# Streams' states renewed in the second mixer, a seven-product down projection in ffn3, merged vector steps and identity products at the start

## The chip, the cores and the metric

The kernel runs on one core of a Trainium2 chip. The metric is the device time of one execution in microseconds (us); below 'the median' is that of three runs. TensorE (PE) multiplies, VectorE (DVE) and ScalarE (ACT) work elementwise, GpSimd (POOL) does small elementwise work and some DMAs, and SyncE (SP) issues nearly all other DMAs. Each engine takes its own instructions in order and waits on semaphores of the others.

## The reference

A streaming encoder of two layers, one inference step for 512 new frames of one stream and 16 frames for each of 8 running streams: 640 tokens of 1024 channels. Each sub-layer ends in `x <- LayerNorm(ALPHA * x + sublayer(x))`:

```python
swiglu:     (silu(x @ w_gate) * (x @ w_up)) @ w_down          # 1024 -> 2816 -> 1024, four times
mixer_ab:   S5 recurrence and stick-breaking attention        # first layer
mixer_ssd:  # second layer; per head r of a group g, 64 rows of state
    xbc  = silu(conv(xbc))                                    # 4 taps, per channel
    cs   = cumsum(dt * a)
    y    = (c @ b.T * exp(cs_t - cs_s) masked * dt) @ x + (c @ h) * exp(cs) + d * x
    h    = h * exp(cs[-1]) + (exp(cs[-1] - cs) * dt * b).T @ x    # new state
    yg   = y * silu(z);  yg = yg * rsqrt(mean(yg ** 2) + eps) * norm_g
    out  = yg @ w_out
```

The outputs are y, the new states of the S5 and SSD recurrences (`ssd_sample`: 8 streams x 32 heads x 64 x 128), keys, values and the last rows of the convolution.

## The kernel before, in words

The order of phases is ffn0, mix0 (first mixer), ffn1, ffn2, mix1 (second mixer), ffn3. Products are in fp32r, with each operand split into a high part and the rest: `split` lets ACT round (`L95`) and DVE subtract (`L96`), and `mm3` (`L134`) makes three products of the pairs. Weights come in pieces of 512 KB through SP into `raw`, are split into `w`, and are used up by PE.

In an FFN the gate and up products of pairs of row blocks f (128 of 2816) are taken by `pair` (`L358`), and `down` multiplies four f at a time into `yacc`. In ffn1 and ffn2 the first five chunks of four f go through `down7` (products `L494`): a two-by-two product of blocks by seven products in place of eight, for four of the five token tiles, with sums of rows (`row_sums`) and of weights on DVE and some results added by POOL's accumulating DMAs (`L506`). ffn0 and ffn3, and the last chunk of each FFN, take eight.

The second mixer works in 4 groups g of 8 heads. For each group six input projections (`xbc`: copy to `ext`, convolution `L1554` to `L1557`, tanh, `L1559`, to memory as `bcx_d`) and four gate projections (`gate_in`, to memory as `z_d`) come first; they are a group ahead of the recurrences and fill in between their steps. A step (g, c) is one token tile c: 4 (the eight running streams) first, then 0 to 3 (the long stream). `core_a` loads `bx` (b, c, x of the tile) and `csb` (the cumulated decay on all partitions), makes the decays (`L1662`, exp `L1664`, `L1670`) and takes b times c on PE (`L1666`, `L1667`). `core_b` multiplies with the running state and renews it (`L1701` to `L1719`); `core_s` does the same for the eight running streams, whose old states `h0` it loads (8 of 128x512 per group, two to a tile). `gate_out` of the group before follows: times z, norm, a split `og` (`L1780`, `L1781`) and 24 products with `w_out` per tile. After the last step only `gate_out(3, c)` and the layer norm are left.

The new states of the running streams are not made in the mixer: it leaves split x and b in memory (`xb_d`) and the decays (`el_d`). `ssd_states`, a generator that is stepped during ffn3, loads them again with h0, takes a product (`L1467`) per group and stream from `xrow` and `brow` (three parts of 16 rows, for two streams at a time, loaded by 12 DMAs), multiplies h0 by its decay and adds (`L1469`, `L1470`).

The order of the instructions on each engine is set when the program is built, by a scheduler that simulates the engines and takes what is ready first, in program order otherwise; `issue_after` pins an instruction behind another one. On the chip that order is fixed.

Of the kernel before, what the change touches and what calls it, by code (L numbers as in the profile page):

```python
# [21 lines left out]
T = 640  # L22
# [8 lines left out]
SEVEN = ("ffn1", "ffn2")  # L31
# [5 lines left out]
def kernel(ctx: ExitStack, tc: tile.TileContext, I, O, phases=PHASES):  # L37
# [31 lines left out]
    def bank_b():  # L69
        return bank("b")  # L70
# [58 lines left out]
    def mm3(ps, lhs, rhs):  # L129
        n = 3 * len(lhs)  # L130
        k = 0
        for (wh, wl), (xh, xl) in zip(lhs, rhs):
            for a, b in ((wh, xh), (wl, xh), (wh, xl)):
                state["pe"] = nc.tensor.matmul(ps, a, b, start=(k == 0), stop=(k == n - 1)).ins  # L134
                k += 1

# [76 lines left out]
    def ffn(i, ph, last, side=None):  # L213
# [4 lines left out]
        with ExitStack() as st:  # L218
# [3 lines left out]
            def tick(where):  # L222
# [1213 lines left out]
    ssd = {}  # L1436

# [5 lines left out]
    def ssd_states(wk):  # L1443

        el8 = wk.tile([128, 4, 8, 8], F32, name="el8")
        nc.sync.dma_start(el8.rearrange("p g b h -> p g (b h)"), ssd["el"])


        xrow = wk.tile([128, 512], F32R, name="xrow", bufs=1)
        brow = wk.tile([128, 2, 128], F32R, name="brow", bufs=1)  # L1450
        nc.vector.memset(xrow.bitcast(F32), 0.0)
        nc.vector.memset(brow.bitcast(F32), 0.0)
        for g, b2, q in ((g, b2, q) for g in range(4) for b2 in range(2) for q in range(2)):
            for h in range(2):
                for r, (sx, sb) in enumerate(((0, 0), (0, 1), (1, 0))):
                    rows = slice(64 * h + 16 * r, 64 * h + 16 * r + 16)
                    t0 = 64 * h + 32 * b2 + 16 * q
                    src = lambda s, a, b: ssd["xb"][g][s, t0:t0 + 16, a:b]
                    nc.sync.dma_start(xrow[rows].bitcast(F32), src(sx, 0, 512))
                    nc.sync.dma_start(brow[rows, h].bitcast(F32), src(sb, 512, 640))  # L1460
            for h in range(2):
                n = 4 * h + 2 * b2 + q
                h0 = wk.tile([128, 512], F32, name="h0", bufs=2)
                nc.sync.dma_start(h0, I["ssd_h0"][g, n])
                yield
                pst = bank_b()
# [520 lines left out]
```

## Time and profile before

| | |
|---|---|
| median of 3 runs | 2546.57 us (2545.01 to 2555.02) |
| profiled execution | 2548.97 us, its span 2547.3 us |
| PE / DVE / ACT / POOL busy | 2501.8 / 2017.0 / 1218.0 / 298.3 us |
| phases, from the span's start | ffn0 to 465.5, mix0 to 762, ffn1 to 1183, ffn2 to 1604.5, mix1 to 2110.2, ffn3 to the end |

Busy time counts an engine's instructions, not its waits. A group's row gives line, engine, operation, tiles, shapes, count, then busy time and the mean duration of one, then the idle time of the engine just before these instructions and what ended it. Matmuls overlap: their spacing, not the mean duration, is what one costs, and an fp32 matmul is two PE instructions.

### The profile page before, as it was taken

The numbers are of one execution on the slowest core, as the hardware profiler recorded it, in microseconds if no ns is written. First come the engines' busy times: TensorE is split into PE (matmuls) and PEld (weight loads), VectorE is DVE, ScalarE is ACT, GpSimd is POOL, SyncE is SP. The second block draws the span as 40 slices with busy tenths as digits, with TensorE's granted clock in tenths as the row PEclk, the third lists the DMA queues.
The fourth block names the chain that finished last, engine by engine and source line by source line (L and its number), as shares of the span: only waits on it lengthen the run. The fifth ranks groups of instructions, "written<-read, shape, count | busy, mean of one in ns | idle before, by whom it ended". The sixth has DMA issues, their size and how long they took to land. (4 is left out here: it accounts for less than half of the span.)

```text
span 2547.3 us, 40681 instructions
## 1 busy us (share of the span) xinstructions
PE 2501.8 (98%) x15577; PEld 2289.1 (90%) x15577; DVE 2017.0 (79%) x3685; ACT 1218.0 (48%) x2309; POOL 298.3 (12%) x432
## 2 busy tenths in 40 slices
PE   9999999999999999999999999999999999999998
PEld 8998999878789999999999999888989879999997
DVE  7787777676778888878888887777686799876768
ACT  4443344336744555553455554566565443443332
POOL 0000001210130000013000002311111150000001
PEclk9999999999999999999999999999999999999999
DMA  5322334443221433452144434366564722543442
GB/s 185 108 92 86 114 117 154 143 150 114 87 76 58 125 103 91 117 156 72 53 114 123 112 103 127 117 189 196 155 204 142 240 74 85 168 147 107 145 140 96
DMA packets 174835, 317.44 MB, mean 125 GB/s; under 512 B 20480, under 2 KB 91776, under 8 KB 174128
## 3 DMA queue, kind: packets, MB, share of 16 engines
q1 hardware_dynamic: 164816, 293.83, 36.2%
q0 software_dynamic: 9824, 21.01, 4.0%
q8 instruction: 122, 2.00, 0.3%
q14 instruction: 73, 0.60, 0.1%
HBM read 259.56 MB, written 40.54 MB: 118 GB/s over the span
## 5 line engine op out<-in xcount | busy, mean ns | idle before, releaser
L96 DVE TENSOR_TENSOR w<-raw,w 128x512 fp32r<-128x512 f32 (+1 forms) x601 | 524.1, 897 | 74.6 <-ACT w L95 73.3
L95 ACT CAST w<-raw 128x512 fp32r<-128x512 f32 (+1 forms) x601 | 441.7, 776 | 286.5 <-PE bank L134 102.7
L358 PE MATMUL bank<-xhi,w 128*128 128x320 f32 x2432 | 540.0, 309 | 1.5 <-ACT mx L369 1.1
L134 PE MATMUL bank<-xhi,w 128*128 128x256 f32 (+2 forms) x2272 | 497.3, 311 | 8.2 <-ACT w L95 6.2
L134 PE MATMUL bank<-w,h 128*128 128x512 f32 x1872 | 436.8, 392 | 0.0
L358 PE MATMUL bank<-T,w 128*128 128x320 f32 x2736 | 426.3, 309 | 1.1 <-DVE s L395 0.7
L134 PEld LDWEIGHTS bank<-w,h 128*128 128x128 f32 x1872 | 350.3, 188 | 73.2 <-DVE h L96 1.0
L358 PEld LDWEIGHTS bank<-xhi,w 128*128 128x128 f32 x2432 | 407.4, 188 | 5.4 <-ACT mx L369 2.3
L358 PEld LDWEIGHTS bank<-T,w 128*128 128x128 f32 x2736 | 406.4, 188 | 3.0 <-DVE s L395 1.3
L134 PEld LDWEIGHTS bank<-xhi,w 128*128 128x128 f32 x2272 | 377.6, 188 | 19.5 <-ACT w L95 6.2
L358 PE MATMUL bank<-xlo,w 128*128 128x320 f32 x1216 | 375.1, 308 | 0.0
L134 PE MATMUL bank<-xlo,w 128*128 128x256 f32 (+2 forms) x1136 | 350.6, 309 | 3.0 <-DVE xlo L198 2.9
L358 PEld LDWEIGHTS bank<-xlo,w 128*128 128x128 f32 x1216 | 228.0, 188 | 0.3
L134 PEld LDWEIGHTS bank<-xlo,w 128*128 128x128 f32 x1136 | 213.8, 188 | 4.4 <-DVE xlo L198 3.6
L210 DVE SCALAR_TENSOR_TENSOR yacc<-bank,yacc 128x512 f32<-128x512 f32 x160 | 109.3, 687 | 76.7 <-PE bank L134 76.2
L369 ACT COPY mx<-bank 128x320 f32<-128x320 f32 x228 | 96.5, 424 | 140.5 <-PE bank L358 140.1
L96 DVE TENSOR_TENSOR w<-sw,w 128x1024 fp32r<-128x1024 f32 x76 | 93.0, 1224 | 53.4 <-ACT w L95 53.0
L95 ACT CAST w<-sw 128x1024 fp32r<-128x1024 f32 x76 | 79.9, 1051 | 98.1 <-DVE sw L337 96.9
L506 POOL DMA_DIRECT2D yacc<-ev x56 | 48.7, 903 | 644.6 <-ACT ev L505 587.8
L134 PE MATMUL bank<-w,og 128*128 128x512 f32 x432 | 104.8, 396 | 2.8 <-DVE og L1781 2.8
L134 PEld LDWEIGHTS bank<-w,og 128*128 128x128 f32 x432 | 79.5, 188 | 20.7 <-DVE og L1781 4.7
L397 ACT ACTIVATE s<-s 128x320 f32<-128x320 f32 x108 | 50.9, 471 | 83.6 <-DVE s L395 83.4
(428 smaller groups left out, 3468.0 us busy)
## 6 DMA issues: line engine op xcount, KB each, us to landing
raw<-in_w_gate_dram SPq DMA_DIRECT2D x88, 512.0 KB, 3.9
raw<-in_w_up_dram SPq DMA_DIRECT2D x88, 512.0 KB, 4.0
raw<-in_w_down_dram SPq DMA_DIRECT2D x88, 512.0 KB, 3.6
raw<-in_m_in_dram SPq DMA_DIRECT2D x52, 512.0 KB, 4.5
yacc<-ev POOLq DMA_DIRECT2D x56, 256.0 KB, 4.3
raw<-in_m_out_dram SPq DMA_DIRECT2D x24, 512.0 KB, 4.1
csb<-cs_d SPq DMA_DIRECT2D x20, 512.0 KB, 5.0
h<-in_ssd_h_dram SPq DMA_DIRECT2D x16, 512.0 KB, 6.2
```

Source lines behind the costliest of these rows:

```text
L95: nc.scalar.copy(hi, src)
L96: return nc.vector.tensor_tensor(lo, src, hi.bitcast(F32), op=ALU.subtract)
L134: state["pe"] = nc.tensor.matmul(ps, a, b, start=(k == 0), stop=(k == n - 1)).ins
L210: state["acc"] = nc.vector.scalar_tensor_tensor(ya, pb, scale, ya, op0=ALU.mult, op1=ALU.add).ins
L358: nc.tensor.matmul(ps, A[p][:, a, k * 128:k * 128 + 128], B[p][b][:, k, :], start=(first and n == 0), stop=(n == 11), skip_group_check=True)
L369: nc.scalar.copy(e[n], ps)
L397: state["silu"] = nc.scalar.activation(t, ps, AF.Silu).ins
L506: nc.gpsimd.dma_start(yacc[:, t, 512 * j:512 * j + 512], e, accum_op=ALU.add)
```

## The change

1. ffn3 takes seven products in its five first chunks (`SEVEN`).
2. The streams' new states are made in the mixer. `core_s` keeps its h0 tiles (`h0s`), the decay tile `e8` stays on chip (`decay`), `el_d` goes. `states_in(g, j)` issues the 12 small loads for two streams, `states_new(g, j)` takes the two products, multiplies on POOL, adds on DVE and writes the state. At a step with c = 4 the first pair is loaded; after the core of the steps 4, 0, 1 and 2 a pair is renewed and the next one loaded. `xrow` and `brow` are set to zero by POOL in the mixer, not by DVE at the start of ffn3. ffn3 has no side work.
3. Steps in the mixer are merged: the convolution runs over all 664 columns at once with the result for the running streams copied out to a tile of its own (`cvs`) and written by a second DMA; the eight subtract-and-min steps of the decay become one subtraction and a Relu on ACT; the norm's gain goes from the rows (`og`, four steps each on ACT and DVE) to the weights (`load_w` with `rows`), so that `og` is one `split`.
4. Eleven fp32 products of the identity with itself come first on PE, and the first real products stand behind them.

```diff
@@ -28,7 +28,7 @@
 PAIRS = 6
-SEVEN = ("ffn1", "ffn2")
+SEVEN = ("ffn1", "ffn2", "ffn3")
 PHASES = ("ffn0", "mix0", "ffn1", "ffn2", "mix1", "ffn3")
@@ -108,13 +108,19 @@
-    def load_w(src):
+    def load_w(src, rows=None):
...
         for j in range(2):
-            split(w[:, j, 0], w[:, j, 1], r[:, 512 * j:512 * j + 512])
+            half = r[:, 512 * j:512 * j + 512]
+            if rows is None:
+                split(w[:, j, 0], w[:, j, 1], half)
+            else:
+                nc.scalar.mul(w[:, j, 0], half, rows)
+                nc.vector.scalar_tensor_tensor(w[:, j, 1], half, rows, w[:, j, 0].bitcast(F32),
+                                               op0=ALU.mult, op1=ALU.subtract)
         return w[:, 0], w[:, 1]
@@ -131,8 +137,10 @@
             for a, b in ((wh, xh), (wl, xh), (wh, xl)):
-                state["pe"] = nc.tensor.matmul(ps, a, b, start=(k == 0), stop=(k == n - 1)).ins
+                with tc.issue_after(state["first"]) if "first" in state else ExitStack():
+                    state["pe"] = nc.tensor.matmul(ps, a, b, start=(k == 0), stop=(k == n - 1)).ins
                 k += 1
+        state.pop("first", None)
@@ -225,9 +233,6 @@
                             next(steps, None)
-                elif ph == "ffn3" and where in ("gate", "up", 0, 2, 4):
-                    with tc.issue_after(state["silu"]):
-                        next(steps, None)
@@ -1433,49 +1438,16 @@
-    def ssd_states(wk):
...
-        el_d = ssd["el"] = dram.tile([128, 4, 64], F32, name="el_d")
-        xb_d = ssd["xb"] = [dram.tile([2, 128, 640], F32, name=f"xb_d{g}") for g in range(4)]
+        xb_d = [dram.tile([2, 128, 640], F32, name=f"xb_d{g}") for g in range(4)]
@@ -1547,17 +1519,21 @@
                     nc.sync.dma_start(O["conv"][:, 6 * g:6 * g + 6], cvo[g])
-                acc = row_tile("acc")[:, :T]
-                win = lambda w: ((ext[:, w:w + 512], acc[:, 0:512]),
-                                 (es_[:, :, w:w + 16], acc[:, 512:640].rearrange("p (b i) -> p b i", i=16)))
-                for i_, o_ in win(0):
-                    nc.scalar.activation(o_, i_, AF.Identity, scale=cw[:, m, 0:1], bias=cw[:, m, 4:5])
+                acc = row_tile("acc")
+                n = 664
+                nc.scalar.activation(acc[:, :n], ext[:, :n], AF.Identity, scale=cw[:, m, 0:1], bias=cw[:, m, 4:5])
                 for w in range(1, 4):
-                    for i_, o_ in win(w):
-                        V.scalar_tensor_tensor(o_, i_, cw[:, m, w:w + 1], o_, op0=ALU.mult, op1=ALU.add)
-                nc.scalar.activation(ext[:, :T], acc, AF.Tanh)
-                V.scalar_tensor_tensor(acc, ext[:, :T], 1.0, acc, op0=ALU.add, op1=ALU.mult)
-                nc.sync.dma_start(bcx_d[g][:, :, u, :], acc.rearrange("p (c t) -> p c t", t=128))
+                    V.scalar_tensor_tensor(acc[:, :n], ext[:, w:w + n], cw[:, m, w:w + 1], acc[:, :n],
+                                           op0=ALU.mult, op1=ALU.add)
+                nc.scalar.activation(ext[:, :n], acc[:, :n], AF.Tanh)
+                runs = lambda t: t[:, 515:667].rearrange("p (b i) -> p b i", i=19)[:, :, :16]
+                last_ = wk.tile([128, 128], F32, name="cvs", bufs=2)
+                V.scalar_tensor_tensor(last_.rearrange("p (b i) -> p b i", i=16), runs(ext), 1.0, runs(acc),
+                                       op0=ALU.add, op1=ALU.mult)
+                V.scalar_tensor_tensor(acc[:, :512], ext[:, :512], 1.0, acc[:, :512], op0=ALU.add, op1=ALU.mult)
+                nc.sync.dma_start(bcx_d[g][:, :4, u, :], acc[:, :512].rearrange("p (c t) -> p c t", t=128))
+                nc.sync.dma_start(bcx_d[g][:, 4, u, :], last_)
@@ -1627,7 +1603,33 @@
-            bl = {}
+            bl, decay, h0s, xb = {}, {}, {}, {}
+            xrow = wk.tile([128, 512], F32R, name="xrow", bufs=1)
+            brow = wk.tile([128, 2, 128], F32R, name="brow", bufs=1)
+            with after_norm():
+                G.memset(xrow.bitcast(F32), 0.0)
+                G.memset(brow.bitcast(F32), 0.0)
+            def states_in(g, j):
+                for h in range(2):
+                    for r, (sx, sb) in enumerate(((0, 0), (0, 1), (1, 0))):
+                        rows = slice(64 * h + 16 * r, 64 * h + 16 * r + 16)
+                        t0 = 16 * (2 * j + h)
+                        nc.sync.dma_start(xrow[rows].bitcast(F32), xb_d[g][sx, t0:t0 + 16, 0:512])
+                        nc.sync.dma_start(brow[rows, h].bitcast(F32), xb_d[g][sb, t0:t0 + 16, 512:640])
+            def states_new(g, j):
+                h0 = h0s.pop((g, j))
+                for h in range(2):
+                    n = 2 * j + h
+                    pst = bank_b()
+                    nc.tensor.matmul(pst, brow[:, h], xrow, start=True, stop=True)
+                    G.tensor_tensor(by_head(h0[:, h]), by_head(h0[:, h]), decay[g][:, n, :, None].to_broadcast(hb3),
+                                    op=ALU.mult)
+                    V.tensor_tensor(h0[:, h], h0[:, h], pst, op=ALU.add)
+                    nc.sync.dma_start(O["ssd_s"][g, n], h0[:, h])
@@ -1646,7 +1648,7 @@
                                          csb.rearrange("p h (b i) -> p h b i", i=16)[:, :, :, 15], AF.Exp)
-                    nc.sync.dma_start(el_d[:, g], e8.rearrange("p b h -> p (b h)"))
+                    decay[g] = e8
                 ecs = None
@@ -1658,10 +1660,9 @@
                     nc.scalar.activation(ecs, tok[:, c, 0, hs], AF.Exp)
-                for h in range(8):
-                    V.tensor_scalar(csb[:, h, :], csb[:, h, :], tok[:, c, 0, 8 * g + h:8 * g + h + 1], 0.0,
-                                    op0=ALU.subtract, op1=ALU.min)
-                nc.scalar.activation(csb, csb, AF.Exp)
+                V.tensor_tensor(csb, csb, tok[:, c, 0, hs, None].to_broadcast([128, 8, 128]), op=ALU.subtract)
+                nc.scalar.activation(csb, csb, AF.Relu, scale=-1.0)
+                nc.scalar.activation(csb, csb, AF.Exp, scale=-1.0)
                 pcb = bank_b()
@@ -1738,7 +1739,7 @@
                 for j in range(4):
-                    h0 = load_h0(wk, g, j)
+                    h0 = h0s[g, j] = load_h0(wk, g, j)
                     for q in range(2):
@@ -1758,7 +1759,7 @@
                 if g not in wo:
-                    wo[g] = [load_w(I["m1_out"][4 * g + k]) for k in range(4)]
+                    wo[g] = [load_w(I["m1_out"][4 * g + k], chp[:, 1, 4 * g + k:4 * g + k + 1]) for k in range(4)]
                 y = ys.pop((g, c))
@@ -1775,11 +1776,7 @@
                 og = wk.tile([128, 4, 2, 128], F32R, name="csb" if g == 3 and c % 2 else "og", bufs=2 if g == 3 and c % 2 else 1)
-                for q in range(4):
-                    ng = chp[:, 1, 4 * g + q:4 * g + q + 1]
-                    nc.scalar.mul(og[:, q, 0], y[:, q], ng)
-                    V.scalar_tensor_tensor(og[:, q, 1], y[:, q], ng, og[:, q, 0].bitcast(F32),
-                                           op0=ALU.mult, op1=ALU.subtract)
+                split(og[:, :, 0], og[:, :, 1], y)
                 for j in range(2):
@@ -1817,8 +1814,15 @@
                         core_a(*steps[i + 1])
+                if c == 4:
+                    states_in(g, 0)
                 (core_b if c < 4 else core_s)(g, c)
                 run_fill(0 if i in (8, 14) else 1)
+                if c != 3:
+                    k = ORDER.index(c)
+                    states_new(g, k)
+                    if k < 3:
+                        states_in(g, k + 1)
                 if g:
@@ -1851,6 +1855,10 @@
+    pw = bank_b()
+    for _ in range(11):
+        state["first"] = nc.tensor.matmul(pw[:, 0:128], ident, ident, start=True, stop=True).ins
     if "mix0" in phases and "ffn0" not in phases:
```

Where the order moves. On SP in the last group (g = 3), where the step (3, 1) is loaded, before: `L1639` is `csb`, `L1634` is `bx`, `L1767` the gate rows z.

```order
L114 DMA raw_21366<-in_w_gate_dram 128x1024
L1579 DMA z_d3_15645<-acc_20508 640x1x128
L1639 DMA csb_20675<-cs_d_15632 128x8x128
L1767 DMA zz_20742<-z_d2_15644 128x512
L1634 DMA bx_20673<-bcx_d3_15636 128x768
L1767 DMA ext_21010<-z_d3_15645 128x512
L1767 DMA acc_21076<-z_d3_15645 128x512
L1767 DMA ext_21138<-z_d3_15645 128x512
L1767 DMA acc_21214<-z_d3_15645 128x512
L114 DMA raw_21373<-in_w_up_dram 128x1024
L1639 DMA csb_20792<-cs_d_15632 128x8x128
L1654 DMA ecs_20679<-cs_d_15632 64x4x128 x2
```

And now (`L1620` and `L1621` are the loads of `states_in`, `L1632` the writes of `states_new`, `L1636` is `bx`, `L1641` is `csb`):

```order
L1632 DMA out_ssd_s_dram<-h0_20439 128x512 x2
L1621 DMA brow_15691<-xb_d3_15652 16x128
L1620 DMA xrow_15690<-xb_d3_15652 16x512
L1621 DMA brow_15691<-xb_d3_15652 16x128
L1620 DMA xrow_15690<-xb_d3_15652 16x512
L1621 DMA brow_15691<-xb_d3_15652 16x128
L1620 DMA xrow_15690<-xb_d3_15652 16x512
L1621 DMA brow_15691<-xb_d3_15652 16x128
L1620 DMA xrow_15690<-xb_d3_15652 16x512
L1621 DMA brow_15691<-xb_d3_15652 16x128
L1636 DMA bx_20800<-bcx_d3_15648 128x768
L1641 DMA csb_20802<-cs_d_15644 128x8x128
```

The loads of the next pair and the writes of the last one stand ahead of `bx` and `csb` of the next step, which had only one load of z between them.

On PE at the same place, the end of step (3, 0) to the start of step (3, 1), before:

```order
L1719 MATMUL bank<-csb,xd 64x128 x8
L1773 MATMUL bank<-ones,zz 128x2
L134 MATMUL bank<-w,og 128x512 x24
L1666 MATMUL bank<-bx 128x128
L1667 MATMUL bank<-ident,bx 128x128
L1676 MATMUL bank<-ident,bx 128x128 x4
L1701 MATMUL bank<-bx,hst 128x128 x4
L1705 MATMUL bank<-xe,bk 128x512
L1719 MATMUL bank<-csb,xd 64x128 x8
```

And now (`L1628` are the states' products, `L141` is `mm3`, `L1667` the product of b and c):

```order
L1720 MATMUL bank<-csb,xd 64x128 x8
L1628 MATMUL bank<-xrow,brow 128x512
L141 MATMUL bank<-w,og 128x512 x3
L1628 MATMUL bank<-xrow,brow 128x512
L141 MATMUL bank<-w,og 128x512 x2
L1774 MATMUL bank<-ones,zz 128x2
L141 MATMUL bank<-w,og 128x512 x19
L1667 MATMUL bank<-bx 128x128
L1668 MATMUL bank<-ident,bx 128x128
L1677 MATMUL bank<-ident,bx 128x128 x4
L1702 MATMUL bank<-bx,hst 128x128 x4
```

The two products of the states come between the core and the output products; the 24 output products then still stand ahead of the next step's `L1667`.

At the start of PE's list, before:

```order
L134 MATMUL bank<-xhi,w 128x256 x2
L134 MATMUL bank<-xlo,w 128x256
L134 MATMUL bank<-xhi,w 128x256 x2
L134 MATMUL bank<-xlo,w 128x256
L134 MATMUL bank<-xhi,w 128x256 x2
```

And now:

```order
L1861 MATMUL bank<-ident 128x128 x11
L141 MATMUL bank<-xhi,w 128x256 x2
L141 MATMUL bank<-xlo,w 128x256
L141 MATMUL bank<-xhi,w 128x256 x2
L141 MATMUL bank<-xlo,w 128x256
```

The products of the first gate block follow the eleven identity products; nothing else moved there.

More of the change, by code (lines that the diff above doesn't have):

```diff
@@ L1433, in mixer0 @@
         state["preload"] = None
-    ssd = {}
     def load_h0(wk, g, j):
@@ L1441, in load_h0 @@
         return h0
-    def ssd_states(wk):
[L1445 to L1466, printed above, removed]
-                nc.tensor.matmul(pst, brow[:, h], xrow, start=True, stop=True)
-                h4 = h0.rearrange("p (h d) -> p h d", d=64)
-                nc.vector.tensor_tensor(h4, h4, el8[:, g, n, :, None].to_broadcast([128, 8, 64]), op=ALU.mult)
-                nc.vector.tensor_tensor(h0, h0, pst, op=ALU.add)
-                nc.sync.dma_start(O["ssd_s"][g, n], h0)
     def mixer1(ph, last):
```

6 lines of the change are left out of this document (removed).

## The prediction

> **What bounds the kernel now.** I read the busy shares first, then the same by phase, then who waited, and last the pieces of the program that the diff touches.
>
> ```profile
> span 2547.3 us, 40681 instructions
> PE 2501.8 (98%) x15577; PEld 2289.1 (90%) x15577; DVE 2017.0 (79%) x3685; ACT 1218.0 (48%) x2309; POOL 298.3 (12%) x432
> ```
>
> TensorE (PE) works 2501.8 of 2547.3 us. What takes products away is therefore worth nearly its whole time, and what takes work off the other engines is worth only the PE idle time that it removes: 45.5 us in all. By phase (columns: window, its length, busy time of PE, PEld, DVE, ACT, POOL, clock, DMA share, GB/s), with the end of the second mixer apart:
>
> ```profile
> 762.00:1183.00 421.00, 420.72 (x2538) 394.60 (x2537) 354.04 (x556) 209.49 (x332) 47.15 (x48) 1.00 0.37 103
> 1604.50:2110.20 505.70, 495.53 (x3243) 443.81 (x3243) 387.74 (x864) 283.11 (x774) 106.33 (x201) 1.00 0.53 165
> 2110.20:2547.00 436.80, 427.15 (x2514) 398.08 (x2512) 341.23 (x535) 156.44 (x266) 10.09 (x8) 0.99 0.40 128
> 2028.00:2060.00 32.00, 29.03 (x178) 21.79 (x173) 29.51 (x73) 16.10 (x50) 12.68 (x16) 1.00 0.52 166
> 2060.00:2110.00 50.00, 46.88 (x259) 39.52 (x259) 45.53 (x91) 23.73 (x46) 28.30 (x28) 1.00 0.19 59
> ```
>
> ffn1 (first row) leaves PE 0.3 us idle in 421. The second mixer leaves 10.2, of which 6.1 lie in the last two rows, where DVE is busy over 90% as well. That end of the mixer has no other work for PE to turn to, and the prediction hangs on it.
>
> **Seven products in ffn3.** ffn1 has them already (first fence), ffn3 has not (second); columns: line, engine, tiles, count, busy us, mean ns.
>
> ```profile
> L134 PE MATMUL bank<-w,h 128*128 128x512 f32 x276 | 64.5, 391 | 0.0
> L494 PE MATMUL bank<-w,hs 128*128 128x512 f32 x192 | 44.2, 389 | 0.0
> L494 PE MATMUL bank<-w,h 128*128 128x512 f32 x144 | 35.1, 393 | 0.0
> ```
>
> ```profile
> L134 PE MATMUL bank<-w,h 128*128 128x512 f32 x660 | 152.7, 390 | 0.0
> L1467 PE MATMUL bank<-xrow,brow 128*128 128x512 f32 x32 | 12.5, 392 | 0.0
> 2149.71 0.23 PE bank L1467
> 2217.21 10.88 PE bank L134 x48
> ```
>
> 276+192+144 = 612 against 660: 48 fewer. In the chain of waits 48 such products take 10.88 us, 0.227 each, so **-10.9 us**. The extra sums and splits on DVE and ACT, and POOL's accumulating DMAs, I cost at nothing: in ffn1 they lie under PE, which idles 0.3 us there. Without that cover the loss would be at most the 10.9 themselves, below.
>
> **States moved from ffn3 into the mixer.** 32 products (L1467, 0.23 each, 7.3 us) leave ffn3 and enter the mixer: 0 net, if PE waits for nothing new. ffn3's DVE is rid of 64 steps, and the states are read from memory once, not twice, but PE did not wait for either there. Only the two memsets stood on the path, between the layer norm and ffn3's first splits:
>
> ```profile
> 2113.16 0.48 DVE xrow L1451
> 2113.65 0.27 DVE brow L1452
> ```
>
> They go to POOL, early in the mixer: **-0.7 us**. In the mixer DVE and ACT change like this (line, tile, count, busy, mean):
>
> ```profile
> L1557 DVE SCALAR_TENSOR_TENSOR acc<-ext,cw,acc 128x512 f32<-128x512 f32 x72 | 53.7, 745 | 17.7 <-POOL cvo L1547 8.6 <-ACT acc L1554 8.0 <-DMA raw<-in_m_in_dram 1.1
> L1557 DVE SCALAR_TENSOR_TENSOR acc<-ext,cw,acc 128x128 f32<-128x128 f32 x72 | 25.3, 351 | 0.0
> L1559 DVE SCALAR_TENSOR_TENSOR acc<-ext,acc 128x640 f32<-128x640 f32 x24 | 19.7, 819 | 2.1 <-ACT ext L1558 2.0
> L1662 DVE TENSOR_SCALAR csb<-csb,tok 128x128 f32<-128x128 f32 x160 | 34.3, 282 | 16.7 <-ACT e L1647 9.6 <-ACT el L1644 6.9
> L1670 DVE TENSOR_TENSOR csb<-csb,cbm 128x1024 f32<-128x1024 f32 x20 | 24.7, 1235 | 0.3
> L1781 DVE SCALAR_TENSOR_TENSOR og<-yb,chp,og 128x128 fp32r<-128x128 f32 x72 | 27.3, 426 | 5.0 <-ACT og L1780 5.0
> L1711 DVE TENSOR_TENSOR hst<-hst,bank 128x512 f32<-128x512 f32 x12 | 8.1, 678 | 0.0
> L1664 ACT ACTIVATE csb<-csb 128x1024 f32<-128x1024 f32 x20 | 21.2, 1058 | 23.9 <-DVE csb L1662 16.7 <-DVE rms L1775 7.1
> L1710 POOL TENSOR_TENSOR hst<-hst,el 128x512 f32<-128x512 f32 x12 | 12.9, 1073 | 78.8 <-DVE hst L1711 54.1 <-ACT hst L1708 24.7
> ```
>
> Convolution: 98.7 us of DVE become 72 steps of 664 columns (745 at 512, 351 at 128, so 1.03 ns a column and 0.90 us) and 24 pairs of 0.7+0.35: 90 us, -9. Decay: 34.3 become 20 steps of L1670's shape, 24.7: -10; ACT gets a Relu of L1664's size, +21 in all. Output rows: 27.3, and 3.5 for the other eight, become 20 steps of about 0.69: -17, and ACT loses about as much. States: 32 adds of 0.68, +22, and 32 multiplies of 1.07 on POOL, +34 on an engine that is busy 106 of 506. Net DVE -14 of 388. This buys only PE idle that DVE causes:
>
> ```profile
> PE bank L134 <- DVE og L1781: 2.8, 3, 2.1
> PE bank L1666 <- DMA bx<-bcx_d: 2.1, 2, 1.1
> ```
>
> I take **-1** of the first row's 2.8 (0 to -2.8); the second row is the place where it gets worse.
>
> **What the move does to SP's queue.** Each state pair brings 12 small loads of `xrow` and `brow`, and two writes of `ssd_s` that wait for DVE's add. SP issues in order. How fast such a burst goes is seen in ffn3 (start, length, queue):
>
> ```profile
> 2243.02 0.42 SPq L1459 DMA_DIRECT2D xrow<-xb_d  x1
> ...
> 2244.41 0.42 SPq L1460 DMA_DIRECT2D brow<-xb_d  x1
> ```
>
> Three issues in 1.39 us, 0.463 apart, whether of 32 KB (`xrow`) or 8 KB (`brow`), so 12 take 5.6. The new order puts the burst ahead of `bx`, the tile that the next step's products need. In the last group a step before went like this (SP, then PE):
>
> ```profile
> 2028.27 0.38 SPq L1639 DMA_DIRECT2D csb<-cs_d  x1
> 2030.21 0.32 SPq L1634 DMA_DIRECT2D bx<-bcx_d  x1
> 2028.40 5.71 PE L134 MATMUL bank<-w,og 128*128 128x512 f32 x24
> 2035.22 0.46 PE L1666 MATMUL bank<-bx 128*128 128x128 f32 x2 [1.11 <-DMA bx<-bcx_d]
> bx<-bcx_d SPq DMA_DIRECT2D x18, 384.0 KB, 4.7
> ```
>
> `bx` was issued at 2030.2 and PE waited 1.1. Now the burst's first load waits for the second state product (L1628), near 2029.4, an output product or three into the row at 2028.40; twelve loads and two waiting writes end near 2035.9, and with 4.7 to land `bx` is there at 2040.6: PE waits 6.3, 5.2 more. Behind it `csb` is late too, and DVE and ACT, in order, hold the rows of the gate output that PE would fill in with. Queued behind the burst's first load on SP are also `zz`, the last gate rows and the first weights of ffn3; behind DVE's add, which waits for L1628, stand the norm of the gate output and its split, for which PE's output products wait. Three such steps give 15.6. Some is given back: before, PE was idle 3.1 in 2060 to 2110, and 24 output products (5.4 us) stand earlier in the new order. I take **+10** (0 where the rows' neighbours cover, +18 where nothing is given back and `csb` adds). The other 13 bursts lie in groups that still have input projections: about 13 to 23 us of products between a burst and the next `bx` at most of them by the order, more than the 12 us that burst and landing need. **+2** (0 to +15, about one us each).
>
> One rule says otherwise. The Trainium skill, "DMA: Bandwidth & Descriptors", section "Issuing engines are not separate DMA queues", holds the sequencer's time to start a DMA for usually small beside the DMA itself. By that rule a late issue would cost next to nothing, the tail term would go to 0 and the sum to that of the first rival below. The rows above differ from it for this kernel: one issue is a tenth of `bx`'s 4.7, but twelve in a row are more than it.
>
> **Warm clock at the start.** Eleven fp32 identity products ahead of the first weights. Before:
>
> ```profile
> 6.15 1.31 PE L134 MATMUL bank<-xhi,w 128*128 128x256 f32 x2 [6.15 <-ACT w L95]
> 7.26 0.41 PE L134 MATMUL bank<-xlo,w 128*128 128x256 f32 x1
> 7.90 0.41 PE L134 MATMUL bank<-xlo,w 128*128 128x256 f32 x1
> 12.38 0.28 PE L134 MATMUL bank<-xlo,w 128*128 128x256 f32 x1
> 12.72 0.28 PE L134 MATMUL bank<-xlo,w 128*128 128x256 f32 x1
> 7.35 2.05 DVE L96 TENSOR_TENSOR xlo<-h,xhi 128x512 fp32r<-128x512 f32 x3
> ```
>
> A triple takes 0.64 until 12.4 and 0.34 after; eight triples, 7.26 to 12.38, would be 2.4 shorter. The splits of `xlo` end at 9.40, so not all of it: **-1.7** (0 to -2.4). The identity is there long before, and the eleven end about when the first weights do.
>
> The rule that bears on it is in the Trainium skill, "TensorE: Matmul & The Clock Gate", part 1: the clock is halved by default and opens after a window of about 3.4 us of sustained work. The rows show 6.2 us from the first product to full speed, with a pause in it. By the rule the clock is open when the first weights come, by the rows it might open a microsecond or two later and the term would be -1.
>
> **Sum**, on the profiled execution of 2548.97: -10.9 -0.7 -1 -1.7 +10 +2 = -2.3, so 2546.7. It stood 2.4 above the median of the runs, 2546.57; as a median, **2544**.
>
> **Rivals.**
>
> *The states are hidden in the mixer.* PE waits for `bx` only 2.1 us in the whole phase although each `bx` takes 4.7 to land, DVE has 14 us less to do, and POOL is three quarters free. Against it: the last group has nothing to cover a burst. Then -10.9 -0.7 -2.8 -1.7 = -16.1: 2530. With a few us left, 2530 to 2536.
>
> *Slower: the burst starves PE throughout.* The place is L1667 of each step, the price the 5.6 us that `bx` is issued later, and it decides as soon as fewer than about 12 us of products stand between a state product and the next L1667. In the last group that is so by the rows; in the first group L1667 stands in the middle, and once in the second 7.5 us stand there. The last three at 5.6 and `csb` with nothing given back, 18, and 1 to 1.5 at each of the 13 others, 16: -13.3 + 34 = +21, 2567. From about +26 of stalls the kernel is slower.
>
> *Seven products do not pay in ffn3.* DVE is at 84% in ffn1 by its row (354 of 421), and ffn3 ends in layer norms that are DVE's. Against: the last chunk keeps the old form. The 10.9 would be lost: 2555.
>
> **How the numbers follow.** Chances: forecast 0.46, hidden 0.31, starved 0.17, seven lost 0.06. A measurement here tells 0.5% (12.7 us) from no change: faster is below 2533.8, slower above 2559.3. Faster: two thirds of hidden and a fourth of the forecast's low side, 0.33; slower: most of starved and a little of the forecast and of the last, 0.20; same 0.47. The forecast's own range, from the tail's 0 to 18, is 2534 to 2555; to hold 8 in 10, 2529 to 2562.
>
> **What would show it.** ffn3 without its states and 48 products shorter by 18 to 19 us (436.8 to about 418); the wait of PE on `bx` (now L1667) grown from 2.1 to over 10 us, at the last group's steps, with SP's twelve loads ahead of it; the first triples at 0.34 from about 7 us on. Wrong: that wait unchanged (hidden), waits on `xrow` or `bx` all over the mixer (starved), or PE idle in ffn3's sums.

## The result, and the profile after

The changed kernel takes 2610.1 us (median of four, 2608.7 to 2613.9) against 2547.2: 2.4% slower, ratio 1.0244 with a 95% interval of 1.0219 to 1.0268. The prediction was 2544, with 2562 as its upper end. The profile after, the page's first rows:

```profile
span 2612.1 us, 40508 instructions
PE 2531.3 (97%) x15551; PEld 2300.9 (88%) x15551; DVE 2031.3 (78%) x3479; ACT 1261.0 (48%) x2289; POOL 370.0 (14%) x494
```

PE has 26 instructions fewer and is busy 29.5 us longer. Where that lies is seen when both kernels are cut at the same instruction, the last transpose of a phase's layer norm. The windows of the second mixer and of ffn3, before (columns as in the prediction):

```profile
1607.90:2114.10 506.20, 497.61 (x3262) 445.86 (x3259) 388.26 (x864) 282.56 (x773) 104.45 (x194) 1.00 0.53 165
2114.10:2547.30 433.20, 423.31 (x2483) 394.44 (x2481) 337.39 (x530) 156.44 (x266) 8.58 (x7) 0.99 0.40 128
```

and after:

```profile
1602.40:2198.20 595.80, 544.00 (x3294) 471.49 (x3292) 390.00 (x650) 288.02 (x713) 152.47 (x230) 0.95 0.52 161
2198.20:2612.10 413.90, 405.46 (x2403) 379.08 (x2401) 349.25 (x537) 194.97 (x308) 32.74 (x35) 0.99 0.36 101
```

The mixer begins 5.5 us earlier and ffn3 is 19.3 shorter, both gains. The mixer itself is 89.6 longer. Its PE idle time grew from 8.6 to 51.8, which is 43 of them. Its mean clock fell from 1.00 to 0.95: the trace has nine stretches of half clock, 65 us together, in which PE was busy for 45, and those products took some 22 us longer than at full clock. The states' products take 7. Another 12 are products of the running streams' core with h0, shown below. The last 4 or 5 lie in spacings of products that I could not put to one cause.

PE's waits in the mixer after, the two largest (us in total, times, longest):

```profile
PE bank L1774 <- POOL zz L1773: 25.1, 6, 7.5
PE bank L1667 <- DMA bx<-bcx_d: 16.8, 3, 7.9
```

The second is the wait that the prediction followed, 2.1 before. The first, the product of the gate's norm (L1774, L1773 before), is one it did not have. The two long waits on `bx` are these:

```profile
1826.90 0.77 PE L1667 MATMUL bank<-bx 128*128 128x128 f32 x2 [7.93 <-DMA bx<-bcx_d]
2101.99 0.77 PE L1667 MATMUL bank<-bx 128*128 128x128 f32 x2 [7.25 <-DMA bx<-bcx_d]
```

The first belongs to step (1, 1), in the second group; the other to step (3, 2), in the last. For the norm's wait the step (3, 4) shows how it comes about. Before, on SP, PE and DVE:

```profile
1991.83 0.33 SPq L1634 DMA_DIRECT2D bx<-bcx_d  x1
1992.20 1.95 SPq L1440 DMA_DIRECT2D h<-in_ssd_h_dram  x3
1994.96 0.41 SPq L1767 DMA_DIRECT2D zz<-z_d  x1
...
2003.33 1.94 PE L1743 MATMUL bank<-h,ctm 128*32 128x512 f32 x16
2007.23 0.68 DVE L1768 TENSOR_TENSOR yb<-yb,zz 128x512 f32<-128x512 f32 x1
2012.65 0.28 PE L1773 MATMUL bank<-ones,zz 128*128 128x2 f32 x2
```

and after:

```profile
2034.96 0.47 SPq L1636 DMA_DIRECT2D bx<-bcx_d  x1
2036.23 0.32 SPq L1620 DMA_DIRECT2D xrow<-xb_d  x1
...
2045.74 0.63 SPq L1621 DMA_DIRECT2D brow<-xb_d  x1
2046.42 1.54 SPq L1443 DMA_DIRECT2D h<-in_ssd_h_dram  x3
2048.57 0.59 SPq L1768 DMA_DIRECT2D zz<-z_d  x1
...
2046.46 1.90 PE L1744 MATMUL bank<-h,ctm 128*32 128x512 f32 x4
2058.30 1.90 PE L1744 MATMUL bank<-h,ctm 128*32 128x512 f32 x4
2066.21 0.69 DVE L1769 TENSOR_TENSOR yb<-yb,zz 128x512 f32<-128x512 f32 x1
2070.41 0.59 PE L1774 MATMUL bank<-ones,zz 128*128 128x2 f32 x2 [7.50 <-POOL zz L1773]
```

Before, three loads of h0 and the load of z followed `bx` within 3.5 us, and the core of the running streams took its 16 products in one go. Now twelve small loads stand between, SP was held up at 2041 to 2045 as well (by a write of gate rows inside the burst, which waited for DVE), and h0 and z are issued 11 to 14 us after `bx`. The core's products are drawn out over nearly 14 us, with gate projections between them that are then used up. They also cost more in themselves: with all h0 tiles there, four products start within 0.05 us of each other and sixteen take 1.94; tile by tile, four take 1.90. In the last three groups together that is 19.1 us where it was 6.7, the 12 named above. DVE's product of y and z stands behind that core in DVE's order, and now behind two adds of states (1.28) and a scaling of weights (1.41) as well, so the norm's product comes 24 us after the core's start where it was 9, and PE, with nothing else left in its list ahead of it, waits 7.5. Up to 2.5 of it can thus be DVE's and not the loads'.

A wait also costs more than its length. The same step in three windows, with the clock in the third column from the end:

```profile
2050.00:2062.00 12.00, 11.82 (x50) 6.47 (x49) 1.80 (x3) 0.72 (x2) 6.13 (x6) 1.00 0.67 242
2062.00:2070.40 8.40, 0.90 (x6) 0.47 (x4) 7.05 (x13) 4.75 (x10) 2.59 (x2) 0.68 0.40 123
2070.40:2078.00 7.60, 7.59 (x26) 6.33 (x27) 1.52 (x3) 1.01 (x1) 1.61 (x2) 0.68 0.87 204
```

and PE's products right after the wait:

```profile
2070.86 1.20 PE L141 MATMUL bank<-w,og 128*128 128x512 f32 x2
2071.85 0.63 PE L141 MATMUL bank<-xhi,w 128*128 128x256 f32 x2
```

During the wait the granted clock falls, and after it PE works on at a lower one: two output products take 0.99 us from start to start, 0.50 each, where 48 such products took 10.88, 0.227 each, before. The Trainium skill, "TensorE: Matmul & The Clock Gate", part 1, states this rule (half clock after an idle window of about 3.4 us, full again after a busy one). The trace agrees for this wait: the clock is 0.68 in the windows of the wait and after it. It does not bear out 3.4 us as the least that a wait must last:

```profile
1879.90 0.38 PE L1774 MATMUL bank<-ones,zz 128*128 128x2 f32 x2 [1.37 <-POOL zz L1773]
1880.90:1884.20 3.30, 3.30 (x17) 3.30 (x17) 1.73 (x3) 0.95 (x2) 0.93 (x1) 0.50 1.05 346
```

Behind a wait of 1.37 us the clock is 0.50 here. So short waits count too.

### The profile page after: what moved, and what is told of

Its sections match the earlier page's. It is cut to its first block, busy times and chain, and to the rows that moved or that the text cites. A ratio compares the mean times of both kernels' runs of the same rounds, so it can differ in the third digit from the quotient of the medians.

```text
span 2612.1 us, 40508 instructions
## 1 busy us (share of the span) xinstructions
PE 2531.3 (97%) x15551; PEld 2300.9 (88%) x15551; DVE 2031.3 (78%) x3479; ACT 1261.0 (48%) x2289; POOL 370.0 (14%) x494
## 5 line engine op out<-in xcount | busy, mean ns | idle before, releaser
L96 DVE TENSOR_TENSOR w<-raw,w 128x512 fp32r<-128x512 f32 (+2 forms) x569 | 519.1, 935 | 77.4 <-ACT w L95 76.5
L141 PE MATMUL bank<-xhi,w 128*128 128x256 f32 (+2 forms) x2272 | 499.0, 311 | 1.3 <-ACT xhi L205 1.0
L141 PEld LDWEIGHTS bank<-xhi,w 128*128 128x128 f32 x2272 | 378.5, 188 | 15.3 <-issue 8.9
L141 PE MATMUL bank<-xlo,w 128*128 128x256 f32 (+2 forms) x1136 | 351.5, 310 | 2.6 <-DVE xlo L206 2.5
L141 PE MATMUL bank<-w,h 128*128 128x512 f32 x1488 | 346.3, 391 | 0.0
L141 PEld LDWEIGHTS bank<-w,h 128*128 128x128 f32 x1488 | 277.1, 188 | 57.0 <-DVE h L96 1.0
L141 PEld LDWEIGHTS bank<-xlo,w 128*128 128x128 f32 x1136 | 213.8, 188 | 7.3 <-issue 3.4
L511 POOL DMA_DIRECT2D yacc<-ev x84 | 72.9, 903 | 965.7 <-ACT ev L510 885.4
L499 PE MATMUL bank<-w,hs 128*128 128x512 f32 x576 | 132.5, 389 | 0.0
L499 PEld LDWEIGHTS bank<-w,hs 128*128 128x128 f32 x576 | 108.1, 188 | 22.4
L141 PE MATMUL bank<-w,og 128*128 128x512 f32 x432 | 117.2, 428 | 3.7 <-DVE og L96 2.5
L507 DVE SCALAR_TENSOR_TENSOR yacc<-bank,yacc 128x512 f32<-128x512 f32 x84 | 57.8, 688 | 66.2 <-PE bank L499 66.2
```

The costliest lines, as they stand in the source:

```text
L96: return nc.vector.tensor_tensor(lo, src, hi.bitcast(F32), op=ALU.subtract)
L499: nc.tensor.matmul(ps, a[:, u], b[:, v], start=(first and n == 0), stop=(n == 5), skip_group_check=True)
L507: V.scalar_tensor_tensor(ya, ps, 0.5 / ALPHA, ya, op0=ALU.mult, op1=ALU.add)
L511: nc.gpsimd.dma_start(yacc[:, t, 512 * j:512 * j + 512], e, accum_op=ALU.add)
```

## Experiments

Each is compared with the kernel before on the same chip. "Mixer" is the window of that run cut as above. Differences between two variants are differences of their medians below; by the ratios they come out up to some 2 us smaller.

**Which part of the change.** The kernel before with the merged steps and the identity products only (`e1_states_stay`: parts 3 and 4); with the states moved and nothing else (`e2_states_only`: part 2); and the changed kernel without the merged steps (`e4_merges_undone`: parts 1, 2 and 4). Each is the diff above, cut to those parts.

> The kernel before with the merged steps of the mixer and the identity products, but the streams' states still made in ffn3 and eight products there. The changed kernel lost 89 us in the mixer (506 to 596) and won 5.4 at the start and 19 in ffn3. Theory Q (the twelve small loads per pair on SP delay bx, h0 and zz, and PE falls to half clock after each stall): the mixer returns to about 500, the whole to about 2540 (2547 less 5.4 and a few us of shorter vector steps). Rival M (the merged steps bring DVE and ACT into an order in which zz and og come late): the mixer stays above 570, the whole above 2600. Rival S (the states' own work in the mixer, the multiplies, adds and kept h0 tiles): as Q.

> The kernel before with the states moved into the mixer and nothing else: no merged steps, no identity products, eight products in ffn3. Q and S: the mixer about 590, ffn3 about 8 us shorter without the states, the whole 2615 to 2640. M: the mixer about 510, the whole 2540 to 2550.

> The changed kernel without the merged steps: convolution in two pieces, eight subtractions per decay, gain in the rows; states in the mixer, seven products in ffn3 and identity products stay. Q and S: the mixer 580 to 610, the whole 2600 to 2625. M: the mixer about 510, the whole about 2530.

| | us | ratio (95%) | mixer |
|---|---|---|---|
| states stay | 2544.9 | 0.9988 (0.9978 to 0.9998) | 508 |
| states only | 2614.3 | 1.0271 (1.0255 to 1.0286) | 582 |
| merges undone | 2604.6 | 1.0230 (1.0215 to 1.0245) | 585 |

The move of the states is the loss, alone and with the rest. Theory M falls. Between the last two runs ffn3 goes from 423.6 us with eight products to 414.2 with seven.

**The loads taken away.** The products, multiplies, adds and writes of the states stay; the loads are made for the first pair only, so later states are made from its rows.

```diff
-                if c == 4:
+                if (g, c) == (0, 4):
                     states_in(g, 0)
...
-                    if k < 3:
-                        states_in(g, k + 1)
```

> The changed kernel with the twelve small loads made once, for the first pair of the first group, and not for the other fifteen pairs (so the later states are made from the first pair's rows; that part of the work is left out). Products, multiplies, adds and writes of the states stay. Q: waits on bx and zz fall to what they were before, the mixer to about 510, the whole to 2525 to 2540. S: the mixer stays above 570, the whole above 2590. M: as S.

2555.2 (1.0034, 1.0021 to 1.0047), mixer 536. Without the later loads 55 of the 63 us are gone. The waits on `bx` are down to 0.4; the norm keeps 9.8:

```profile
PE bank L1774 <- POOL zz L1773: 9.8, 3, 4.0
PE bank L141 <- DVE og L96: 3.1, 1, 3.1
```

The expected 2525 to 2540 was missed: the rest of the states' work costs as well.

**Number, queue or place.** Four variants of the changed kernel: two pairs per load, so half as many; each pair's loads written after the next `core_a`; the loads issued by ACT; the multiplies on DVE.

```diff
# half the loads
-            xrow = wk.tile([128, 512], F32R, name="xrow", bufs=1)
-            brow = wk.tile([128, 2, 128], F32R, name="brow", bufs=1)
+            xrow = wk.tile([128, 2, 512], F32R, name="xrow", bufs=1)
+            brow = wk.tile([128, 2, 2, 128], F32R, name="brow", bufs=1)
...
-                        nc.sync.dma_start(xrow[rows].bitcast(F32), xb_d[g][sx, t0:t0 + 16, 0:512])
+                        src = lambda s, a, b: xb_d[g][s, :, a:b].rearrange("(j h i) c -> h i j c", h=2, i=16)[h, :, j:j + 2]
+                        nc.sync.dma_start(xrow[rows].bitcast(F32), src(sx, 0, 512))
...
-                    if k < 3:
-                        states_in(g, k + 1)
+                    if k == 1:
+                        states_in(g, 2)
# later: behind core_a of the next step, ahead of the step's own core
-                if c == 4:
-                    states_in(g, 0)
+                if c != 3:
+                    states_in(g, ORDER.index(c))
...
-                    if k < 3:
-                        states_in(g, k + 1)
# ACT's queue (brow alike)
-                        nc.sync.dma_start(xrow[rows].bitcast(F32), xb_d[g][sx, t0:t0 + 16, 0:512])
+                        nc.scalar.dma_start(xrow[rows].bitcast(F32), xb_d[g][sx, t0:t0 + 16, 0:512])
# multiplies on DVE
-                    G.tensor_tensor(by_head(h0[:, h]), by_head(h0[:, h]), decay[g][:, n, :, None].to_broadcast(hb3),
+                    V.tensor_tensor(by_head(h0[:, h]), by_head(h0[:, h]), decay[g][:, n, :, None].to_broadcast(hb3),
```

> The changed kernel with the small loads made for two pairs at once: the same bytes in 24 loads per group, not 48, and two waits per group for the product that frees the tiles, not four. So far, without the later loads the mixer took 536 us, with them 596. If the number of issues on SP sets the loss (theory Q), about half of those 60 us comes back: the mixer 560 to 570, the whole 2575 to 2585. If what counts is the place of a burst just before bx or h0, whatever its length, less comes back: 2590 to 2605.

> The changed kernel with each pair's loads written after the next step's bx and csb in the program, not before them; nothing else moves in the program. If the place ahead of bx is what costs (Q), PE's waits on bx fall from 17 us to a few and the whole to 2560 to 2585; the states' products then come later. If the loss is the time that SP is taken up altogether, little changes: 2595 to 2610.

> The changed kernel with the small loads issued by ACT, not SP. Q: SP's queue is as free as without the loads, so the mixer falls towards 536 and the whole towards 2555, less what ACT loses by 192 issues of about 0.4 us (77 us on an engine that is idle half the time, but in order): 2555 to 2590. If the transfers themselves (traffic, landing) cost, and not the queue: 2600 or more.

> The changed kernel with the states' multiplies on DVE, as ffn3 had them, not on POOL. PE's waits for the gate's norm end on POOL (25 us, six times). If the multiplies in POOL's queue delay the norm (part of rival S), those waits fall to a few us and the whole to 2575 to 2590. If POOL only comes last in a chain that is late for other reasons (Q), the whole stays at 2600 to 2620.

| | us | ratio (95%) | mixer |
|---|---|---|---|
| half the loads | 2593.8 | 1.0190 (1.0173 to 1.0207) | 575 |
| later | 2604.7 | 1.0227 (1.0209 to 1.0245) | 580 |
| ACT's queue | 2593.6 | 1.0188 (1.0172 to 1.0204) | 570 |
| multiplies on DVE | 2610.9 | 1.0256 (1.0240 to 1.0272) | 589 |

None gives back more than 17 us, so neither the number of issues nor the queue as such nor POOL is the cause by itself. Half the loads, later loads and the multiplies came out in the range expected if Q, as it stood, or the rival about POOL were wrong; ACT's queue, at 2593.6, between its two ranges. The second run shows why; its waits of PE:

```profile
PE bank L1774 <- POOL zz L1773: 32.8, 6, 9.1
PE bank L1628 <- DMA xrow<-xb_d: 5.1, 1, 5.1
...
PE bank L1667 <- DMA bx<-bcx_d: 0.5, 1, 0.5
```

The wait on `bx` is gone (16.8 to 0.5), but the norm's grew from 25.1 to 32.8: in that kernel the first burst of a group still stands ahead of h0 and z, and 22 of the 32.8 are at the first steps of the last three groups. The delay had only changed its place. With ACT's queue it is alike: the waits on `bx` fall to 2.0 and the norm's rise to 30.6, which fits that ACT, in order, makes the norm's squares behind the loads it issues. This led to theory P: what counts is what stands behind a burst, and h0 and z count like `bx`.

**The state work behind all of it.** Loads and products at the end of the step, behind the core and the gate output; the same with products a step later (`e9_pend`); with the merged steps undone (`e9_end_nm`); and with those undone and half the loads (`e10_half_end_nm`).

```diff
-                if c == 4:
-                    states_in(g, 0)
                 (core_b if c < 4 else core_s)(g, c)
                 run_fill(0 if i in (8, 14) else 1)
-                if c != 3:
-                    k = ORDER.index(c)
-                    states_new(g, k)
-                    if k < 3:
-                        states_in(g, k + 1)
                 if g:
                     gate_out(g - 1, c)
+                if c != 3:
+                    states_in(g, ORDER.index(c))
+                    states_new(g, ORDER.index(c))
```

> The changed kernel with the state work of a step, loads and products, written at the end of the step, after the core and the gate output; nothing left out. In the runs so far the first burst of a group stands ahead of the h0 and z loads on SP (2036 to 2046), core_s is drawn out from 1.4 to 13 us, the norm's product comes 26 us after b times c where it was 12, and PE waits there 5 to 12 us in every variant but the one without later loads. Theory P (place: h0, z and bx behind a burst): PE's waits on zz fall below 8 us and those on bx below 3, the mixer to 525 to 545, the whole to 2540 to 2560. If the count of loads and the single pair of tiles cost wherever they stand: the whole stays at 2585 or more.

> The changed kernel with the loads at the end of a step and the products at the end of the next one, so that no product waits for its loads. P with a free wait for landing: as the run with both at the end or up to 10 us below it, 2530 to 2555. If h0 tiles that are given back a step later delay the next group's h0 loads: 2560 or more, with PE waiting on h0.

> The same with the merged steps of the mixer undone. With the states in the mixer the merged steps cost 5.5 us of the whole so far (2610 against 2604.6). P: 2535 to 2560, and up to 10 below the run with merged steps; if the merges are worth their DVE time once the waits are gone, above it.

> Merged steps undone, state work at the end of the step, and loads for two pairs at once (24, not 48, per group). If issues still cost beside their place, this is 5 to 20 us below the run with 48 loads, and could be below the kernel before (2547): 2525 to 2545.

| | us | ratio (95%) | mixer |
|---|---|---|---|
| at the end | 2565.7 | 1.0079 (1.0061 to 1.0097) | 545 |
| products a step later | 2563.3 | 1.0062 (1.0046 to 1.0078) | 543 |
| at the end, merges undone | 2578.1 | 1.0123 (1.0107 to 1.0139) | 558 |
| that, half the loads | 2570.7 | 1.0094 (1.0078 to 1.0110) | 549 |

The same work, with the same loads on the same queue, is 44 us cheaper when it is written last: some 70% of the loss of 63. At the step (3, 4) the loads of h0 and z now start within 3.5 us of that of `bx`, ahead of the burst, and the core's sixteen products are together again:

```profile
2006.49 0.43 SPq L1636 DMA_DIRECT2D bx<-bcx_d  x1
2006.98 1.83 SPq L1443 DMA_DIRECT2D h<-in_ssd_h_dram  x3
2009.92 0.65 SPq L1768 DMA_DIRECT2D zz<-z_d  x1
2010.61 0.43 SPq L1620 DMA_DIRECT2D xrow<-xb_d  x1
...
2018.01 1.94 PE L1744 MATMUL bank<-h,ctm 128*32 128x512 f32 x16
```

P holds for most of the loss, not for all of it: the time was missed by 6, and the norm's waits, forecast below 8, are 18.4. The wait on `bx` is gone from the largest:

```profile
PE bank L1774 <- POOL zz L1773: 18.4, 5, 6.0
PE bank L1750 <- DVE xe L1747: 2.5, 3, 1.8
```

With the state work behind, the merged steps save 12 us; with it in front they cost 5.5, but there the intervals of the ratios overlap. Both runs without them missed their ranges. Half the loads saved 7, as expected, but did not come below the kernel before. Products a step later are the same as without (the intervals overlap); PE waits 1.4 on h0 there.

**What is left.** The changed kernel without any state work (`e15_no_states`; the new states are left out); and, of the kernel with it at the end, one with the first burst only (later states made from its rows) and one without state work in the last group (its states left out). Last, the kernel before with the identity products alone. The first three edits are shown against the kernel with the state work at the end.

```diff
# no state work
-                if c != 3:
-                    states_in(g, ORDER.index(c))
-                    states_new(g, ORDER.index(c))
# at the end, one burst
-                    states_in(g, ORDER.index(c))
+                    if (g, c) == (0, 4):
+                        states_in(0, 0)
# at the end, not in the last group
-                if c != 3:
+                if c != 3 and g < 3:
```

> The changed kernel with the streams' new states left out altogether (neither loads, nor products, multiplies, adds and writes); seven products in ffn3, merged steps and identity products stay. It measures the other parts of the change together. If the states are the whole loss: the mixer 506 to 510 as with the states in ffn3, ffn3 405, the whole 2520 to 2528.

> The kernel with the state work at the end of a step, with only the first of the sixteen bursts of loads (the later states are made from the first pair's rows). With all loads it took 2565.7, mixer 545. If what is left of the loss comes from the bursts (zz behind them in the last group): 2530 to 2545, mixer 510 to 525. If from the products, multiplies, adds and the h0 tiles that are held: 2555 to 2566.

> The kernel with the state work at the end of a step, without any state work in the last group (its 8 states are left out, a quarter of that work). If the rest of the loss sits where no input projections are left to fill in (the last group), as the prediction had it: 2538 to 2550. If it is spread over the groups: 2555 to 2562.

> The kernel before with the eleven identity products at the start and nothing else. With them ffn0 ended 3 to 5 us earlier in the profiles, 2 of it in the first products. If that is kept: 2541 to 2544 against 2547; if it is noise of a stall later in ffn0: 2545 to 2547.

| | us | ratio (95%) | mixer |
|---|---|---|---|
| no state work | 2526.1 | 0.9922 (0.9909 to 0.9936) | 509 |
| at the end, one burst | 2552.6 | 1.0020 (1.0007 to 1.0033) | 530 |
| at the end, not in the last group | 2546.1 | 0.9993 (0.9984 to 1.0002) | 526 |
| identity products alone | 2541.4 | 0.9981 (0.9972 to 0.9989) | 507 |

The window of the mixer without state work:

```profile
1601.10:2109.70 508.60, 499.55 (x3261) 449.04 (x3260) 363.36 (x618) 287.04 (x713) 116.57 (x198) 0.99 0.53 165
```

The states cost 84 us where the change put them (2610.1 less 2526.1) and 40 at the end of a step; 7 of either are their products, which ffn3 had to pay for as well. Cut by kind, the later loads are 13 of the 40; cut by place, half, 20, is the last group's. The runs with one burst show what the move to the end is worth without the loads: 2555.2 in front, 2552.6 at the end, 3 us. So some 42 of the 44 us are the place of the loads. What the other parts give is 21, of which 7 are the states' products that this kernel leaves out: 14, the sum of the prediction's 10.9, 0.7, 1 and 1.7, though not term by term (below). The 27 that stay without loads are 7 of products and 20 that I did not divide further among the adds, the multiplies, the writes and the h0 tiles that are held longer; in the profiled run, 6 us quicker than the median, they are 21. The time with one burst lies between the two ranges expected of it.

Of all kernels that compute everything, the one before with eleven identity products has the lowest median: 2541.4. A kernel with the states in ffn3 and seven products there was not tried.

## Why the prediction was wrong

- **Seven products in ffn3** (-10.9, with the states and memsets some -19 in ffn3): right. ffn3 is 19.3 shorter: 9.6 by the states' leaving (423.6 with the states moved and nothing else), and 9.4 more with seven products as well. The third rival (seven products that do not pay) falls.
- **Start** (-1.7, 0 to -2.4): the clock opened as forecast; that the gain came out larger is luck. The first rows after:

```profile
5.59 1.06 PE L1861 MATMUL bank<-ident 128*128 128x128 f32 x4
6.96 0.28 PE L141 MATMUL bank<-xlo,w 128*128 128x256 f32 x1
7.31 0.28 PE L141 MATMUL bank<-xlo,w 128*128 128x256 f32 x1
```

  The first triple takes 0.35 at 7 us where it took 0.64; two of the next take 0.54 and 0.46. The doubt whether the clock would open in time was idle: the rule of the Trainium skill quoted there held, not my reading of the rows. Counted in PE's order, the products at 54 us are 1.9 earlier than before, but those at 87 us only 0.8, behind a new wait of 0.9 at 74.6. With the identity products alone they are 0.5 earlier and then 0.9 later. So what the warm clock won is mostly spent by 87 us. The gain came later in ffn0, in both runs: a wait of 1.3 us at 205 with half clock behind it, and one of 1.1 at 397, are gone. Why they went is not shown. Alone the start is worth 4.8 us by the ratio (2.8 to 7.1), 5.5 in the profile of the changed kernel.
- **Merged steps** (-1): within what the runs tell when the states stay in ffn3 (2544.9 against 2541.4 without, intervals that overlap). With the state work at the end they save 12; why is not shown. DVE, which they were to relieve, is as busy in the mixer as before (388.3 and 390.0; forecast -14): the convolution's steps take 0.95 each, not 0.90, and DVE scales the weights.
- **The tail** (+10, 0 to +18): the place was right, the mechanism in one step out of three, the size not. The forecast's three steps follow the norm's product of step (3, 4), at 2012.65 before and 2070.41 after (shown above). From there to the end of the mixer PE has the same products, but for 6 of the states, and takes 101.4 us before and 127.8 after: +26, of which 1.4 are those products and some 2 the half clock left by the wait at 2070. Of three waits on `bx` one came, 7.25 where 6.3 was forecast. As long were waits that the forecast did not have: 7.32 for the norm at 2134.45, and the half clock, since it priced waits at their length alone.
- **The other 13 bursts** (+2, 0 to +15): this is the step that failed. The last group begins, by the norm's product at the end of the step before it, at these rows before and after:

```profile
1987.88 0.38 PE L1773 MATMUL bank<-ones,zz 128*128 128x2 f32 x2
```

```profile
2031.01 0.38 PE L1774 MATMUL bank<-ones,zz 128*128 128x2 f32 x2
```

  Up to there 43.1 us are lost on the clock of the trace, 48.6 against the earlier start, 5.5 of it products: +43. The thirteenth burst is the one of step (3, 4), 39.4 us long where it was 24.8 with the same projections, half a us of it products: +14. Together these bursts cost some 57, not 2. The rule by which they were covered, products enough between a burst and the next `bx`, asked only about `bx`. At a group's first step nothing of it holds: the core of the running streams needs h0, the norm needs z, and both stood behind the burst. "Queued behind the burst's first load on SP are also `zz`" stands in the prediction, but only for the last group and without a price; h0 is not in it. And for `bx` itself the cover was short once, with 7.93 at step (1, 1): about 5 us of projections stood between the state products and the wait, where 12 were needed by the forecast's own count (it had found 7.5 at one place of that group).
- **The rivals.** "The burst starves PE throughout" had a chance of 0.17 and 2567. It is the nearest, with the right place in the queue, but too few things behind it: it is 43 us short. "Hidden" is what moving the work would have had to reach; even at the end of a step it does not. The rule of the Trainium skill, "DMA: Bandwidth & Descriptors", "Issuing engines are not separate DMA queues", by which starting a DMA is usually short beside the DMA, agrees with one load here, 0.46 us beside the 4.7 of `bx`. It does not carry over to a burst of twelve ahead of loads that PE needs: half the loads or another queue gave 14 to 16 us each.

## What to carry to other kernels

Before small transfers are moved into a queue that works in order, list every load that will stand behind them, not only the one that already waits; here the place of the state work was worth 44 us, nearly all of it the place of its loads, and more than halving the loads or changing the queue. On an engine that is busy 98% price a wait by its length and by the clock that it costs afterwards. Where a change moves work out of a phase that covers it, first measure that phase without the work: the 14 us to be won were less than half of the 33 that the move cost, beyond the states' own products, at its best place found.

## What the runs showed of the hardware

A wait of PE of 7.5 us is followed by products at half clock (0.50 us in place of 0.227 for 512 columns), and so is one of 1.37 us; in the mixer such stretches add up to 65 us, with the ends of the waits in them, and cost some 22 beyond the waits themselves. Sixteen products with stationary tiles of 32 columns take 1.94 us when all their operands are there, as four at a time run side by side, and 4 times 1.90 when the operands come one by one. Twelve loads of 32 and 8 KB took SP 5.6 us again at 0.46 each, but with waits inside the burst up to 10 (2036.2 to 2046.4). Twenty-two passes of a 128-column fp32 identity product, from 1.6 to 6.6 us, were enough to open the clock for the first real products; that they pay is not shown by this, since the gain of that run came later.
